# Attention projections 512 columns wide, dealt out behind chosen scores

## The chip, the cores and the metric

The kernel runs on one core of one Trainium2 chip. The metric is the device time of one execution in microseconds (us). Its work is done by TensorE (PE in the profile, with the weight loads shown apart as PEld), VectorE (DVE), ScalarE (ACT), GpSimd (POOL) and SyncE (SP, which here only starts transfers); transfers between memory and the core's on-chip buffer run on 16 DMA engines. Each engine takes its own instructions strictly in the order in which they stand in its program, and waits for the others by semaphores.

## The reference

The program is one inference step of a two-layer streaming trunk over 512 prompt frames and 8 running streams of 16 frames, so 640 rows of width 1024. Layer 0 mixes with a chunked gMLP and a short convolution, layer 1 with a forgetting attention (FoX); each is followed by a SwiGLU feed-forward with a short convolution. The change touches layer 1's attention alone:

```
def _fox_project(x, w_in, b_f, q_norm, k_norm):
    z = x @ w_in
    q, k, v, f = jnp.split(z, [D_C, 2 * D_C, 3 * D_C], axis=-1)
    q = _rmsnorm(q.reshape(b, t, C_HEADS, C_HEAD_DIM), q_norm)
    k = _rmsnorm(k.reshape(b, t, C_HEADS, C_HEAD_DIM), k_norm)
    ...
def _fox_attend(q, k, v, dq, dk, q_pos, k_pos):
    s = einsum('bthd,bshd->bhts', q, k) * (C_HEAD_DIM ** -0.5)
    s = s + swapaxes(dq, 1, 2)[..., :, None] - swapaxes(dk, 1, 2)[..., None, :]
    p = softmax(where(k_pos <= q_pos, s, NEG_INF))
    return einsum('bhts,bshd->bthd', p, v)
```

There are 16 heads of 64. The prompt attends causally to itself in blocks of 128 queries; each stream attends to 256 cached rows and its own 16. The keys and values of the new rows are outputs too, and the attention's output goes through one projection (`w_out_c`) onto the residual stream.

## The kernel before, in words

Activations are kept as 8 chunks of 128 features by 640 rows. For accuracy every large product is taken three times, from a high part (a cast) and a low part (the remainder) of each operand: high by high, low by high, high by low. A weight tile is 128x1024; `weights` loads it on SP's queue, casts it on ACT (L94) and subtracts on DVE (L95). Elsewhere (`weights_added`, `weights_down`) the low part is made as the negated high part on ACT (L103) onto which a DMA from POOL's queue adds the raw weights once more (L104, L122), so that DVE has no part in it.

The attention goes over 4 groups of 4 heads. `project` makes q, k and v of a group, one after the other, each 256 columns wide: 5 blocks of 128 rows times 24 matmuls of 128x256 (L696), so 60 walks and 1440 matmuls in all; ACT evicts each block with the row's norm (L699), and q and k are normed per head (squares on ACT, sums and the products on DVE, the power on POOL, L704 to L710). A weight tile holds the 256 columns for half the features, so a kind has two of them.

Each group has two pairs of heads. `operands` transposes q and k of a pair (L726) and makes for each of its heads four score operands: `qa` and `ka` from ACT (L733, L736), half of `qa` and of `kb` copied to other partitions by DMAs on SP's queue (L734, L737), `qb` and the rest of `ka` from DVE (L735, L738), and the rows of the forget terms by two more DMAs. `stream_operands` does so for the streams (L791 to L798). Then come the steps of the pair in the text's order "b30", "s0", "b31", "o", "b20", "s1", "b21", "b10", "b11", "b00", "b01": b and two digits is `prompt_block` of query block 3 to 0 and head 0 or 1 (score L758 and L759, mask L760, maximum L778, exponential L780, reciprocal L781, scaling L783, transposes L765, copy L768 on DVE for odd blocks or L770 on ACT for even ones, product with v L772), s is a pair of streams, o makes the operands of the second pair. `prompt_end` copies the pair's result out (L750). After the groups stands the output projection, 8 blocks of 128x320 matmuls (`po`, L251).

The text is not the order that runs. A list scheduler sets each engine's static order ahead of time, by the text's position as priority and its own model of when each instruction could start. So matmuls of the next group's projection (for the last group: of the output projection) stand wherever the scheduler saw TensorE free. One construct overrides it: what is written under `tc.issue_after(x)` is held behind instruction x.

Of the kernel before, what the change touches and what calls it, by code (L numbers as in the profile page):

```python
# [53 lines left out]
class Core:  # L54
# [52 lines left out]
    def weights_added(self, src):  # L107
        raw = self.raw()
        self.nc.sync.dma_start(out=raw, in_=src)
        return self.added(self.wp, ("whi", "wlo"), raw, src, 1024, 1024)  # L110
# [453 lines left out]
class Attention:  # L564
# [108 lines left out]
    def project(self, g, h, first, after_q=None):  # L673

        k, nc, io = self.k, self.nc, self.io
        z = []
        for kind in range(3):
            if kind == 1 and after_q is not None:
                after_q()
            us = [k.weights(io["w_c"][g, kind, u]) for u in range(2)]  # L680
            zt = self.zp.tile([P, 5, 256], F32, tag="qk" if kind < 2 else "v", name=k.nm("z"), bufs=3 if kind < 2 else 2)
            z.append(zt)
            bank, out = [], []
            for tb in range(5):
                if tb % 2 == 0:
                    bank.append(self.pj.tile([P, 512], F32, tag="pj", name=k.nm("pj")))
                out.append(bank[tb // 2][:, (tb % 2) * 256:(tb % 2) * 256 + 256])
            walk = [(0, 2), (1, 3), (4,)] if first and kind == 0 else [(tb,) for tb in range(5)]
            for tbs in walk:
                for kc in range(8):  # L690
                    wh, wl = us[kc // 4]
                    hh, hl = h[kc]
                    c = (kc % 4) * 256
                    for tb in tbs:
                        for i, (l, r) in enumerate(((hh, wh), (hl, wh), (hh, wl))):
                            nc.tensor.matmul(out[tb], lhsT=l[:, tb * P:(tb + 1) * P], rhs=r[:, c:c + 256],  # L696
                                             start=kc == 0 and i == 0, stop=kc == 7 and i == 2)
            for tb in range(5):
                nc.scalar.activation(out=zt[:, tb, :], in_=out[tb], func=AF.Copy, scale=self.rt[:, tb:tb + 1])  # L699
            if kind < 2:  # L700
                ss = self.zp.tile([P, 20], F32, tag="ss", name=k.nm("ss"))
                for tb in range(5):
                    sq = self.zp.tile([P, 256], F32, tag="sq", name=k.nm("sq"))
                    nc.scalar.activation(out=sq, in_=zt[:, tb, :], func=AF.Square)  # L704
                    nc.vector.reduce_sum(out=ss[:, tb * 4:tb * 4 + 4], in_=sq.rearrange("p (h d) -> p h d", d=64), axis=AX.X)
                    k.rstd_of(ss[:, tb * 4:tb * 4 + 4], ss[:, tb * 4:tb * 4 + 4], 1.0 / 64)
                zh = zt.rearrange("p t (h d) -> p (t h) d", d=64)
                nc.vector.tensor_tensor(out=zh, in0=zh, in1=ss.unsqueeze(2).broadcast_to([P, 20, 64]), op=ALU.mult)
                if kind == 1:
                    nc.vector.tensor_tensor(out=zh, in0=zh, in1=self.cst[:, O_KN:O_KN + 64].unsqueeze(1).broadcast_to([P, 20, 64]), op=ALU.mult)  # L710
            if kind:
                nc.scalar.dma_start(out=io["o_kv"][kind - 1, :, :, 256 * g:256 * g + 256].rearrange("t p c -> p t c"), in_=zt)
        return z
# [38 lines left out]
    def prompt_block(self, g, pair, hh, i, z):  # L752
# [6 lines left out]
        nc.tensor.matmul(s[:, 0:n], lhsT=qb[0:68, i * P:n], rhs=kb[0:68, 0:n], start=False, stop=True)  # L759
# [26 lines left out]
    def stream_operands(self, g, z):  # L786
# [5 lines left out]
        kt = self.sp.tile([P, 256], F32, tag="kts", name=k.nm("kts"))  # L792
# [21 lines left out]
    def streams_pair(self, g, sp, z, ops):  # L814
# [3 lines left out]
        ck = self.sp.tile([P, 1024], F32, tag="ckv", name=k.nm("ck"), bufs=3)  # L818
        nc.sync.dma_start(out=ck, in_=io["c_k"][g, sp])
        cv = self.sp.tile([P, 1024], F32, tag="ckv", name=k.nm("cv"), bufs=3)  # L820
# [32 lines left out]
        on = self.sp.tile([P, P], F32, tag="on", name=k.nm("on"))  # L853
# [9 lines left out]
def build(ctx, tc, io):  # L863
# [73 lines left out]
    def decay():  # L937
        with ExitStack() as ds:
            k.tp = k.pool(ds, "tmpb", bufs=9)
            at.constants()  # L940
            at.decay(h, ds)
        at.open(es)
    for g in range(4):
        z = at.project(g, h, g == 0, decay if g == 0 else None)
        if g == 3:
            o = [k.split(k.hp, HT_, at.o[c]) for c in range(6)]
        sops = at.stream_operands(g, z)
        at.streams_start(g)
        for pair in range(2):
# [3 lines left out]
            for st in ("b30", "s0", "b31", "o", "b20", "s1", "b21", "b10", "b11", "b00", "b01"):  # L953
# [9 lines left out]
    cut = [6, 6, 6, 6, 6, 4, 4, 4]  # L963
    for ob in (6, 7, 0, 1, 2, 3, 4, 5):
        n = cut[ob]
        w = k.weights(io["w_oc"][ob, :, 0:n * P], n * P)
        ps_ = [at.pj.tile([P, 512], F32, tag="pj", name=k.nm("po")) for _ in range(2)]
# [126 lines left out]
```

## Time and profile before

| | us |
|---|---|
| median of 3 runs (from, to) | 1527.41 (1525.31, 1528.93) |
| the profiled execution | 1525.84 |
| its span, first to last instruction | 1524.0 |
| PE busy | 1471.2 (97%) |
| DVE busy | 1047.9 (69%) |
| ACT busy | 736.9 (48%) |
| POOL busy | 211.1 (14%) |
| mean granted TensorE clock | 0.986 of full speed |

The attention's projections and groups stand between about 670 and 1034 us of the span. Busy time is that in which an engine has an instruction in work; PE's is modelled at its ends, since matmuls are pipelined. A row of the timeline or the chain starts with the time from the span's start and a length in us; behind the names, in brackets, stands the idle time ahead of the instruction and what ended it. Rows of groups have the count (x), the busy time in us and the mean of one in ns.

### The profile page before, as it was taken

The page shows a single profiled execution, that of the slowest core. Times are in us where ns is not written, and L with a number is a line of the kernel's source. Part 1 is how long each engine was busy: PE and PEld are TensorE (multiplying, and loading weights), DVE is VectorE, ACT ScalarE, POOL GpSimd, SP SyncE. Part 2 cuts the span into 40 slices and gives each one's busy share as a digit, 9 for nine tenths or more (in the row PEclk, how much of TensorE's full clock was granted, in tenths as well). Part 3 has the DMA queues.
Part 4 walks back from the last instruction along what each step waited for, and adds up shares of the span by engine and source line. Part 5 has one row for each costly group of instructions (what it writes and reads, how often), then busy time and mean ns, then how long its engine had stood idle before and what let it go on. Part 6 is the DMA issues. An engine that isn't in the chain of part 4 may idle for free.

```text
span 1524.0 us, 26325 instructions
## 1 busy us (share of the span) xinstructions
PE 1471.2 (97%) x10576; PEld 1418.3 (93%) x10576; DVE 1047.9 (69%) x1805; ACT 736.9 (48%) x1326; POOL 211.1 (14%) x235
## 2 busy tenths in 40 slices
PE   8999997899999999999999999999699999999998
PEld 6999997899999999989988888888699999999998
DVE  6555438777877777586666657668777686868764
ACT  5422325555555555445544445435455555545551
POOL 4100121101010101135101111003111010101010
PEclk9999998999999999999999999999899999999999
DMA  7222203444444444453534333432254454545342
GB/s 269 77 76 67 67 29 82 133 112 115 106 117 101 115 108 114 81 171 130 171 111 145 109 110 103 161 105 73 54 144 98 99 127 99 127 98 127 97 103 81
DMA packets 74249, 168.04 MB, mean 110 GB/s; under 512 B 13760, under 2 KB 22896, under 8 KB 74000
## 3 DMA queue, kind: packets, MB, share of 16 engines
q1 hardware_dynamic: 49392, 133.79, 27.9%
q0 software_dynamic: 12032, 25.17, 10.4%
q10 hardware_dynamic: 12704, 7.41, 1.6%
q8 instruction: 83, 1.36, 0.4%
q14 instruction: 38, 0.31, 0.1%
HBM read 150.58 MB, written 11.54 MB: 106 GB/s over the span
## 4 chain that ended last, share of the span: by engine, by line
PE 90%; DVE 3%; issue 2%; DMA 2%; ACT 2%; SPq 0%; POOL 0%; DVEq 0%; POOLq 0%
PE mm L251 37%; PE zx L201 20%; PE pj L696 11%; PE aux L201 8%; PE pv L772 3%; PE po L251 2%; PE pt L765 1%; DVE hl L282 1%; PE mm L389 1%; DVE wlo L95 1%; DMA wlo<-w_up 1%; PE pt L851 1%; PE sc L758 1%; PE sc L759 1%; PE scs L830 1%
## 5 line engine op out<-in xcount | busy, mean ns | idle before, releaser
L135 ACT CAST sh<-raw 128x1024 fp32r<-128x1024 f32 (+2 forms) x152 | 142.4, 943 | 192.3 <-PE zx L201 105.4
L251 PE MATMUL mm<-sh,wlo 128*128 128x320 f32 x872 | 203.5, 310 | 5.9 <-ACT sn L216 3.1
L251 PE MATMUL mm<-sh,whi 128*128 128x320 f32 x872 | 200.9, 310 | 2.7 <-ACT sh L135 1.7
L251 PE MATMUL mm<-sl,whi 128*128 128x320 f32 x872 | 199.1, 309 | 0.6 <-DVE sl L136 0.6
L136 DVE TENSOR_TENSOR sl<-raw,sh 128x1024 fp32r<-128x1024 f32 (+2 forms) x152 | 165.0, 1091 | 45.2 <-ACT sh L135 31.0
L348 DVE SCALAR_TENSOR_TENSOR t<-zp,cst,t 128x656 f32<-128x656 f32 x184 | 163.6, 896 | 29.1 <-ACT t L346 28.5
L201 PE MATMUL zx<-hh,sh 128*128 128x320 f32 x576 | 178.2, 309 | 2.0 <-ACT sh L135 1.3
L201 PE MATMUL zx<-hl,sh 128*128 128x320 f32 x576 | 177.8, 309 | 0.0
L201 PE MATMUL zx<-hh,sl 128*128 128x320 f32 x576 | 177.6, 308 | 0.0
L251 PEld LDWEIGHTS mm<-sh,wlo 128*128 128x128 f32 x872 | 147.5, 189 | 6.4 <-ACT sn L216 3.3
L94 ACT CAST whi<-raw 128x1024 fp32r<-128x1024 f32 (+3 forms) x94 | 80.1, 856 | 149.6 <-PE mm L251 85.8
L251 PEld LDWEIGHTS mm<-sh,whi 128*128 128x128 f32 x872 | 146.3, 188 | 4.6 <-ACT sh L135 2.4
L251 PEld LDWEIGHTS mm<-sl,whi 128*128 128x128 f32 x872 | 146.1, 188 | 1.1 <-DVE sl L136 1.1
L696 PE MATMUL pj<-whi,hl 128*128 128x256 f32 x480 | 137.3, 287 | 3.1 <-DVE hl L282 3.1
L359 DVE TENSOR_TENSOR x<-mm,x 128x640 f32<-128x640 f32 x111 | 91.2, 822 | 69.3 <-PE mm L251 69.0
L696 PE MATMUL pj<-wlo,hh 128*128 128x256 f32 x480 | 137.2, 286 | 0.0
L696 PE MATMUL pj<-whi,hh 128*128 128x256 f32 x480 | 136.7, 287 | 0.0
L251 PE MATMUL mm<-hh,whi 128*128 128x320 f32 x512 | 120.3, 317 | 10.4 <-ACT whi L102 10.4
L251 PE MATMUL mm<-hh,wlo 128*128 128x320 f32 x512 | 118.5, 314 | 10.9 <-DMA wlo<-w_up 10.9
L251 PE MATMUL mm<-hl,whi 128*128 128x320 f32 x512 | 119.4, 315 | 2.0 <-DVE hl L282 2.0
L95 DVE TENSOR_TENSOR wlo<-raw,whi 128x1024 fp32r<-128x1024 f32 (+3 forms) x94 | 101.6, 1084 | 23.5 <-ACT whi L94 23.3
L201 PEld LDWEIGHTS zx<-hh,sh 128*128 128x128 f32 x576 | 108.5, 188 | 2.8 <-ACT sh L135 1.5
(232 smaller groups left out, 3350.5 us busy)
## 6 DMA issues: line engine op xcount, KB each, us to landing
raw<-w_up SPq DMA_DIRECT2D x88, 512.0 KB
raw<-w_dn SPq DMA_DIRECT2D x40, 512.0 KB
wlo<-w_dn POOLq DMA_DIRECT2D x40, 512.0 KB, 5.9
raw<-w_c SPq DMA_DIRECT2D x24, 512.0 KB
raw<-w_ab SPq DMA_DIRECT2D x16, 512.0 KB
ck<-c_k SPq DMA_DIRECT2D x16, 512.0 KB
cv<-c_v SPq DMA_DIRECT2D x16, 512.0 KB
o_kv<-z ACTq DMA_DIRECT2D x8, 640.0 KB
```

Of the source, the lines that this page charges most:

```text
L94: nc.scalar.copy(out=hi[:, c], in_=raw[:, c])
L95: nc.vector.tensor_tensor(out=lo[:, c], in0=raw[:, c], in1=hi[:, c].bitcast(F32), op=ALU.subtract)
L135: nc.scalar.copy(out=hi, in_=src)
L136: nc.vector.tensor_tensor(out=lo, in0=src, in1=hi.bitcast(F32), op=ALU.subtract)
L201: nc.tensor.matmul(out, lhsT=l[:, c], rhs=r, start=start and p == 0 and i == 0, stop=p == 3 and i == 2, skip_group_check=True)
L251: nc.tensor.matmul(outs[h], lhsT=l, rhs=r[:, h * HT:(h + 1) * HT], start=start and k == 0, stop=stop and k == 2)
L282: nc.vector.scalar_tensor_tensor(out=lo, in0=x, scalar=gs, in1=hi.bitcast(F32), op0=ALU.mult, op1=ALU.subtract)
L348: nc.vector.scalar_tensor_tensor(out=cv[:, 0:CW], in0=zp[:, i:i + CW], scalar=w[:, i:i + 1], in1=cv[:, 0:CW], op0=ALU.mult, op1=ALU.add)
L359: self.nc.vector.tensor_tensor(out=x, in0=ps[:, C0:C0 + T], in1=x, op=ALU.add)
L389: nc.tensor.matmul(pvs[tb], lhsT=l[:, tb * P:(tb + 1) * P], rhs=r[:, (kc % 2) * 512:(kc % 2 + 1) * 512], start=kc == 0 and k == 0, stop=kc ...
L696: nc.tensor.matmul(out[tb], lhsT=l[:, tb * P:(tb + 1) * P], rhs=r[:, c:c + 256], start=kc == 0 and i == 0, stop=kc == 7 and i == 2)
L772: nc.tensor.matmul(ov[64 * hh:64 * hh + 64, i * P:n], lhsT=z[2][:, j, (2 * pair + hh) * 64:(2 * pair + hh) * 64 + 64], rhs=u[:, j * P:(j + ...
```

## The change

q and k of a group are projected together, 512 columns wide (`project_qk`), and v of two groups together (`project_v`). A walk is one block of 128 rows by 512 columns: 24 matmuls of 128x512. There are 4 x 5 walks for q and k and 2 x 5 for v, less joined ones in the first group, so 720 matmuls. Each projection has four weight tiles, each with the 512 columns for a quarter of the features; the buffers stay at five for the high and five for the low parts. The first group's q and k and the first v are projected ahead of the loop with `weights`; the other 16 tiles and the 8 of the output projection now come by `weights_added`.

The rest of the projection and the output projection's blocks are no longer left to the scheduler's filling. They are 28 steps in `queue`, and the tables `share` and `after` say behind which scores of which pair the next step's TensorE work is held: two, three or four steps for a pair, never one behind b00 or b01 and none ahead of b30. Eviction and norms are now per walk and 512 wide; a q and k tile is normed in one product of 2560 columns on DVE. Some buffer counts change.

```
-    def weights_added(self, src):
+    def weights_added(self, src, cols=1024):
...
+        return self.added(self.wp, ("whi", "wlo"), raw, src, 1024, cols)
-    def project(self, g, h, first, after_q=None):
...
-                if tb % 2 == 0:
-                    bank.append(self.pj.tile([P, 512], F32, tag="pj", name=k.nm("pj")))
...
-                            nc.tensor.matmul(out[tb], lhsT=l[:, tb * P:(tb + 1) * P], rhs=r[:, c:c + 256],
...
+    def walk(self, us, h, tbs, evict):
+        k, nc = self.k, self.nc
+        out = [self.pj.tile([P, 512], F32, tag="pj", name=k.nm("pj")) for _ in tbs]
+        for kc in range(8):
+            wh, wl = us[kc // 2]
+            hh, hl = h[kc]
+            c = (kc % 2) * 512
+            for tb, o in zip(tbs, out):
+                for i, (l, r) in enumerate(((hh, wh), (hl, wh), (hh, wl))):
+                    nc.tensor.matmul(o, lhsT=l[:, tb * P:(tb + 1) * P], rhs=r[:, c:c + 512],
+                                     start=kc == 0 and i == 0, stop=kc == 7 and i == 2)
+        for tb, o in zip(tbs, out):
+            evict(tb, o)
+
+    def project_qk(self, g, h, pairs=False):
...
+        zt = self.zp.tile([P, 5, 512], F32, tag="qk", name=k.nm("z"), bufs=2)
+        ss = self.zp.tile([P, 40], F32, tag="ss", name=k.nm("ss"))
+
+        def evict(tb, o):
+            nc.scalar.activation(out=zt[:, tb, :], in_=o, func=AF.Copy, scale=self.rt[:, tb:tb + 1])
+            sq = self.zp.tile([P, 512], F32, tag="sq", name=k.nm("sq"), bufs=1)
+            nc.scalar.activation(out=sq, in_=zt[:, tb, :], func=AF.Square)
+            s = ss[:, tb * 8:tb * 8 + 8]
+            nc.vector.reduce_sum(out=s, in_=sq.rearrange("p (h d) -> p h d", d=64), axis=AX.X)
+            k.rstd_of(s, s, 1.0 / 64)
+            if tb < 4:
+                return
+            zh = zt.rearrange("p t (h d) -> p (t h) d", d=64)
+            nc.vector.tensor_tensor(out=zh, in0=zh, in1=ss.unsqueeze(2).broadcast_to([P, 40, 64]), op=ALU.mult)
+            zk = zt[:, :, 256:512].rearrange("p t (h d) -> p t h d", d=64)
+            nc.vector.tensor_tensor(out=zk, in0=zk, in1=self.cst[:, O_KN:O_KN + 64].unsqueeze(1).unsqueeze(1).broadcast_to([P, 5, 4, 64]), op=ALU.mult)
+            nc.scalar.dma_start(out=io["o_kv"][0, :, :, 256 * g:256 * g + 256].rearrange("t p c -> p t c"), in_=zt[:, :, 256:512])
+        us = []
+        def step(tbs):
+            if not us:
+                us.extend((k.weights_added if g else k.weights)(io["w_qk"][g, u]) for u in range(4))
+            self.walk(us, h, tbs, evict)
+        walk = [(0, 1), (2, 3), (4,)] if pairs else [(tb,) for tb in range(5)]
+        return (zt[:, :, 0:256], zt[:, :, 256:512]), [lambda tbs=tbs: step(tbs) for tbs in walk]
+
+    def project_v(self, gg, h):
+
+        k, nc, io = self.k, self.nc, self.io
+        zs = [self.zp.tile([P, 5, 256], F32, tag="v", name=k.nm("z"), bufs=3) for _ in range(2)]
+
+        def evict(tb, o):
+            for i, zt in enumerate(zs):
+                nc.scalar.activation(out=zt[:, tb, :], in_=o[:, 256 * i:256 * i + 256], func=AF.Copy, scale=self.rt[:, tb:tb + 1])
+                if tb == 4:
+                    g = 2 * gg + i
+                    nc.scalar.dma_start(out=io["o_kv"][1, :, :, 256 * g:256 * g + 256].rearrange("t p c -> p t c"), in_=zt)
+        us = []
+        def step(tb):
+            if not us:
+                us.extend((k.weights_added if gg else k.weights)(io["w_vc"][gg, u]) for u in range(4))
+            self.walk(us, h, (tb,), evict)
+        return zs, [lambda tb=tb: step(tb) for tb in range(5)]
+        score = nc.tensor.matmul(s[:, 0:n], lhsT=qb[0:68, i * P:n], rhs=kb[0:68, 0:n], start=False, stop=True)
+        return score
...
+    cut = [6, 6, 6, 6, 6, 4, 4, 4]
+    def out_block(ob):
+        n = cut[ob]
+        w = k.weights_added(io["w_oc"][ob, :, 0:n * P], n * P)
+        ps_ = [at.pj.tile([P, 512], F32, tag="pj", name=k.nm("po")) for _ in range(2)]
+        for kc in range(n):
+            k.mm([p_[:, 0:HT] for p_ in ps_], w, kc, o[kc], kc == 0, kc == n - 1)
+        if ob < 6:
+            nc.sync.dma_start(out=x[ob], in_=io["s_x"][ob])
...
+    qk, steps = at.project_qk(0, h, True)
+    for f in steps:
+        f()
+    decay()
+    v, steps = at.project_v(0, h)
+    for f in steps:
+        f()
+
+    share = {(0, 0): 3, (0, 1): 4, (1, 0): 4, (1, 1): 4, (2, 0): 3, (2, 1): 2, (3, 0): 4, (3, 1): 4}
+    after = {2: ("b30", "b21"), 3: ("b30", "b31", "b21"), 4: ("b30", "b31", "b21", "b11")}
+    qks = {}
+    queue = []
     for g in range(4):
-        z = at.project(g, h, g == 0, decay if g == 0 else None)
-        if g == 3:
+        z = qk + (v[g],)
+        if g == 0:
+            for i in (1, 2):
+                qks[i], steps = at.project_qk(i, h)
+                queue += steps
+            vs, steps = at.project_v(1, h)
+            v += vs
+            queue += steps
+        elif g == 1:
+            qks[3], steps = at.project_qk(3, h)
+            queue += steps
+        elif g == 3:
             o = [k.split(k.hp, HT_, at.o[c]) for c in range(6)]
+            queue += [lambda ob=ob: out_block(ob) for ob in (6, 7, 0, 1, 2, 3, 4, 5)]
         sops = at.stream_operands(g, z)
...
-                    at.prompt_block(g, pair, int(st[2]), int(st[1]), z)
+                    score = at.prompt_block(g, pair, int(st[2]), int(st[1]), z)
+                    if st in after[share[g, pair]]:
+                        with tc.issue_after(score.ins):
+                            queue.pop(0)()
             at.prompt_end(g, pair)
...
-        w = k.weights(io["w_oc"][ob, :, 0:n * P], n * P)
...
+        qk = qks.get(g + 1)
+    assert not queue
```

Left out are the smaller buffer counts (q and k tiles 3 to 2 of double width, v tiles 2 to 3, cached rows `ckv` 3 to 2, `kts` and `on` 2 to 1) and the new packing of the weights ahead of the run. In the changed program's numbering the score's two matmuls are L777 and L778, the operand transposes L745, `qa` L752, `ka` L755, the stream operands L811 and L818, the probabilities' transposes L784, the products with v L791, the projection L683, and the evictions L695 (q, k) and L723 (v).

Three places show how the engines' programs change; rows are "line, operation, output, inputs, shape", and the numbers in the names tell tiles apart.

On TensorE before, from the end of group 0 to the first score of group 1 (`pt_1125` and `pt_1126` take the transposed q and k of the new pair, `pj` is the projection, `sc` the score):

```order
L772 MATMUL pv_1014_7619<-u_1080_7865,z_921_7154 64x128
L726 MATMUL pt_1125_8366<-cst_66,z_1087_7881 128x128
L726 MATMUL pt_1126_8371<-cst_66,z_1103_8049 128x128 x4
L696 MATMUL pj_1287_8948<-whi_1280_8935,hl_815_6447 128x256
...
L696 MATMUL pj_1288_8949<-whi_1280_8935,hl_808_6419 128x256
L758 MATMUL sc_1136_8401<-ka_1128_8377,qa_1127_8376 128x512
```

Between the last operand transpose and the score stand 46 projection matmuls; at the starts of groups 0 and 2 there are 43 and 37, and at that of group 3 output projection in their place.

The same place on TensorE after the change, from the last two scores of group 0 to the first of group 1:

```order
L777 MATMUL sc_1120_8001<-ka_989_7414,qa_988_7413 128x128
L778 MATMUL sc_1120_8001<-kb_991_7416,qb_990_7415 128x128
L875 MATMUL pt_1077_7814<-cst_66,on_1079_7832 128x128
L791 MATMUL pv_1039_7613<-u_1105_7932,z_907_6988 64x128 x2
L791 MATMUL pv_1039_7613<-u_1111_7950,z_907_6988 64x128 x2
L784 MATMUL pt_1118_7996<-cst_66,p_1115_7989 128x128
L784 MATMUL pt_1124_8012<-cst_66,p_1121_8005 128x128
L811 MATMUL pt_1128_8020<-cst_66,z_926_7151 128x128 x4
L791 MATMUL pv_1039_7613<-u_1119_7998,z_907_6988 64x128
L745 MATMUL pt_1130_8037<-cst_66,z_926_7151 128x128 x4
...
L745 MATMUL pt_1131_8042<-cst_66,z_926_7151 128x128 x4
L777 MATMUL sc_1141_8072<-ka_1133_8048,qa_1132_8047 128x512
```

No projection matmul stands in this stretch any more: the score follows the transposes directly, and so it does at the starts of the other three groups. The next step's matmuls (`pj_1147`) come behind the score's second half.

On ACT after the change, from the next-to-last walk of the first v (`pj_924`) to the first pair's `qa` (`whi_955` to `whi_961` belong to the next q and k, `whi_1087` to the ones after it):

```order
L723 ACTIVATE z_908_6989<-pj_924_7095,rt_853_6598 128x256
L102 CAST whi_955_7240<-raw_954_7238 128x1024 [waits DMAHW2_49,PE_49]
L103 ACTIVATE wlo_956_7241<-whi_955_7240 128x1024 [waits DMASW2_49,PE_49,Activation_49]
L102 CAST whi_958_7247<-raw_957_7245 128x1024 [waits PE_49]
L102 CAST whi_961_7254<-raw_960_7252 128x1024 [waits PE_49]
L103 ACTIVATE wlo_959_7248<-whi_958_7247 128x1024 [waits DMASW7_49,Activation_49]
L102 CAST whi_1087_7861<-raw_1086_7859 128x1024 [waits DMAHW5_49,PE_49]
L103 ACTIVATE wlo_962_7255<-whi_961_7254 128x1024 [waits DMASW6_49,Activation_49]
L723 ACTIVATE z_907_6988<-pj_925_7122,rt_853_6598 128x256 [waits PE_49]
L723 ACTIVATE z_908_6989<-pj_925_7122,rt_853_6598 128x256
L752 ACTIVATE qa_936_7184<-pt_934_7174,qn8_6619 64x512 [waits DMAHW0_49,DMAHW7_49,DVE_49,PE_49]
```

Seven casts and negations of weights stand ahead of `qa`; before, `qa` of the first pair stood directly behind the eviction of an earlier walk of v, with no weight cast between. `PE_49` in the brackets is the release of the weight buffer, which the last walk of v still reads.

More of the change, by code (lines that the diff above doesn't have):

```diff
@@ L105, in added @@
         return hi, lo
-    def weights_added(self, src):
-        raw = self.raw()
+    def weights_added(self, src, cols=1024):
+        raw = self.raw()[:, 0:cols]
         self.nc.sync.dma_start(out=raw, in_=src)
-        return self.added(self.wp, ("whi", "wlo"), raw, src, 1024, 1024)
+        return self.added(self.wp, ("whi", "wlo"), raw, src, 1024, cols)
     def weights_down(self, src, n):
```

63 lines of the change are left out of this document (11 added, 52 removed).

## The prediction

> **What bounds the kernel now.** I read the busy times first, then the chain of work that ended last, then busy time by stretches around the attention.
>
> ```profile
> PE 1471.2 (97%) x10576; PEld 1418.3 (93%) x10576; DVE 1047.9 (69%) x1805; ACT 736.9 (48%) x1326; POOL 211.1 (14%) x235
> PE 90%; DVE 3%; issue 2%; DMA 2%; ACT 2%; SPq 0%; POOL 0%; DVEq 0%; POOLq 0%
> ```
>
> TensorE is busy for 97% of the span and makes 90% of the chain. The stretches (columns: from and to, length, then busy time and count on PE, PEld, DVE, ACT and POOL, granted clock, DMA share, GB/s) say where it is not:
>
> ```profile
> 670.00:685.00 15.00, 12.12 (x84) 11.07 (x83) 15.00 (x10) 8.32 (x12) 13.38 (x11) 1.00 0.32 112
> 685.00:978.00 293.00, 290.84 (x2590) 260.54 (x2591) 194.86 (x523) 146.59 (x352) 50.52 (x47) 1.00 0.42 131
> 978.00:1034.00 56.00, 55.42 (x483) 47.24 (x482) 39.13 (x129) 20.91 (x62) 0.17 (x3) 0.98 0.29 93
> ```
>
> The attention's start waits for VectorE (15.00 of 15). From 685 to 1034 us TensorE is idle 2.16 + 0.58 = 2.7 us. So work off TensorE is worth nothing there: whatever ACT or DVE save is not on the chain. The change can win only by cheaper matmuls and the start, and lose by every wait that it opens.
>
> **What it wins.** The chain shows how fast each form goes back to back (start, length, line, count):
>
> ```profile
> 694.52 17.28 PE pj L696 x144
> 712.45 14.39 PE pj L696 x120
> ...
> 31.86 2.72 PE mm L389 x12
> 36.17 2.73 PE mm L389 x12
> ```
>
> The 128x256 form takes 17.28/144 = 0.120 us. A 128x512 form of the same weights by rows exists in layer 0: 2.72/12 = 0.227 us. The projections go from 1440 x 0.120 = 172.8 to 720 x 0.227 = 163.4 us: **-9.4**.
>
> [...]
>
> At the start, the high and low parts of the input come from DVE chunk by chunk:
>
> ```profile
> 677.70 0.38 PE L696 MATMUL pj<-whi,hl 128*128 128x256 f32 x1 [1.15 <-DVE hl L282]
> ...
> 679.80 0.39 PE L696 MATMUL pj<-whi,hl 128*128 128x256 f32 x1 [0.25 <-DVE hl L282]
> ...
> 681.91 0.38 PE L696 MATMUL pj<-whi,hl 128*128 128x256 f32 x1 [0.23 <-DVE hl L282]
> ```
>
> These waits and one behind them are within the 15.00 - 12.12 = 2.9 us idle there. Twice the work per chunk (q and k at once) fills them: **-2.9**; bounds 0 (DVE as late as the work is longer) and -2.9.
>
> At the start of group 3 the filling output projection was itself late:
>
> ```profile
> 970.11 1.49 ACT L798 ACTIVATE qbd<-pt,qn 64x128 f32<-64x128 f32 x4 [1.89 <-DVE kts L793]
> ...
> 971.63 0.59 ACT L750 COPY x<-pv 128x512 f32<-128x512 f32 x1
> ...
> 972.24 0.68 ACT L733 ACTIVATE qa<-pt,qn 64x512 fp32r<-64x512 f32 x1
> ...
> 972.95 0.54 SPq L734 DMA_DIRECT2D qa<-qa  x1
> ...
> 974.07 0.56 PE L251 MATMUL po<-sh,whi 128*128 128x320 f32 x2 [1.24 <-ACT sh L135]
> ...
> 975.34 0.47 PE L758 MATMUL sc<-ka,qa 128*128 128x512 f32 x1 [0.71 <-DVE sl L136]
> ```
>
> That is 1.24 + 0.71 = **-2.0**, since no output projection stands there any more. Together -14.3. Fewer changes between forms may give something that no row isolates; the projection's weight loads lose a little to issue, which bounds it at 3 x 1.8 = 5.4 (one row of three alike):
>
> ```profile
> L696 PEld LDWEIGHTS pj<-wlo,hh 128*128 128x128 f32 x480 | 91.5, 191 | 2.0 <-issue 1.8
> ```
>
> I take 0.
>
> **What it loses at the three changes of group.** Before, 46 projection matmuls (5.5 us) stood between the operand transposes and the first score. After, nothing does, and the last two blocks b00 and b01 of the group have no step behind them either. The 128-wide softmax chain:
>
> ```profile
> L780 ACT ACTIVATION_READ_ACCUMULATOR p<-sc,m 128x1 f32 x64 | 12.7, 198 | 0.0
> L778 DVE TENSOR_REDUCE m<-sc 128x1 f32<-128x128 f32 x16 | 4.5, 287 | 0.2
> L780 ACT ACTIVATE p<-sc,m 128x128 f32<-128x128 f32 x16 | 5.9, 370 | 6.4 <-DVE m L778 5.3 <-PE pt L765 0.9
> L783 DVE TENSOR_SCALAR p<-p,l 128x128 f32<-128x128 f32 x16 | 4.4, 284 | 0.3
> L781 DVE RECIPROCAL l<-l 128x1 f32<-128x1 f32 x80 | 12.1, 157 | 7.7 <-ACT p L780 7.0 <-ACT pp L780 0.2
> ```
>
> With a mask as long as the maximum, 0.29 + 0.29 + 0.37 + 0.20 + 0.16 + 0.28 = 1.6 us, and about 0.4 more for the second head: 2.0 from score to probabilities, which stand ahead of the new transposes on TensorE. Then the rows above: qbd 1.49, the pair's copy 0.59, `qa` 0.68, and 975.34 - 972.95 = 2.4 from the issue of its DMA to the score, 5.2 together. Of 7.2, TensorE's own products and transposes in the stretch (some 20 small ones) cover 1.1 to 1.8. Idle: 5.4 to 6.1, I take **6 each, +18**. Bounds: with qbd and the copy behind `qa`, 2.0 + 0.7 + 2.4 - 1.8 = 3.3 each, 10; with nothing covered and, in group 3, the norm of its q and k not yet done (a product of 2560 columns is two of the row below), 3 x 7.2 + 3.0 = 25.
>
> ```profile
> L708 DVE TENSOR_TENSOR z<-z,ss 128x1280 f32<-128x1280 f32 x8 | 11.9, 1485 | 2.6 <-POOL ss L302 2.6
> ```
>
> **What it loses at the first group.** Seven casts and negations of weights now stand ahead of `qa` on ACT:
>
> ```profile
> L94 ACT CAST whi<-raw 128x1024 fp32r<-128x1024 f32 x60 | 62.5, 1048 | 109.8 <-PE mm L251 67.2 <-issue 27.0 <-DMA raw<-w_ab 6.5
> L699 ACT ACTIVATE z<-pj,rt 128x256 f32<-128x256 f32 x60 | 25.7, 472 | 37.1 <-PE pj L696 32.1 <-DVE ss L301 3.5 <-DMA t<-sel 1.3
> L103 ACT ACTIVATE wlo<-whi 128x1024 fp32r<-128x1024 f32 x8 | 8.4, 1054 | 0.0
> ```
>
> Their buffers come free over the last walk of v (24 x 0.227 = 5.4 us), the fourth at its end. From there: a cast 1.05, a negation 1.05, two evictions 0.94, `qa` 0.68, its DMA 2.4 = 6.1; TensorE has 1.8 of transposes. Idle 4.3, and the score's second half waits for `ka` behind qbd; I take **+5**. Bounds: 3 if the fourth buffer is free earlier, 7.4 if all seven run after the walk and only transposes lie beside them.
>
> **Weights.** Four tiles a projection and five buffers: a new tile can be made only while the old projection's last walk runs. At each of the turnovers inside the queue a tile costs a cast 1.05, a negation 1.05, the POOL issue and the landing:
>
> ```profile
> L122 POOL DMA_DIRECT2D wlo<-w_dn x40 | 48.3, 1208 | 177.4 <-ACT wlo L121 167.5 <-ACT t L495 9.9
> wlo<-w_dn POOLq DMA_DIRECT2D x40, 512.0 KB, 5.9
> wlo<-w_up POOLq DMA_DIRECT2D x8, 512.0 KB, 8.3
> ```
>
> 1.05 + 1.05 + 5.9 = 8.0 us if the landing counts from the issue (9.2 with the issue's 1.2), against the 5.4 us of a walk and the attention's own work until the next step. From qk1 to qk2 about 2.5 late; from qk2 to v1 the last step of the one (behind b11) and the first of the other (behind b30) have a change of group between them. I take **+3**; bounds 0 and 7. Behind a waiting cast on ACT stand exponentials, so a late release delays a softmax too.
>
> [...]
>
> **Uncovered blocks.** Pairs with two or three steps leave b31 or b20, b10, b11 without cover: (0,0), (2,0), (2,1). Two or three chains of the 1.6 to 2.0 us above, partly beside other blocks: **+5**, bounds 0 and 9.
>
> **The clock after waits.**
>
> ```profile
> 970.00:980.00 10.00, 8.05 (x50) 5.51 (x48) 5.88 (x12) 5.59 (x11) 0.00 (x0) 0.83 0.39 109
> 1095.00:1105.00 10.00, 2.02 (x8) 1.62 (x7) 9.52 (x17) 4.37 (x6) 2.93 (x4) 0.50 0.92 207
> ```
>
> Around the group-3 start the clock was granted at 0.83 of full speed for 10 us, a loss of 1.7 us, though TensorE was idle only 2 us there; after a long wait it was 0.50. Four such starts: 4 x 1.7 = **+7**, bounds 0 and 14 (twice as long). [...]
>
> **Sum.** -14.3 + 18 + 5 + 3 + 5 + 7 = +23.7 against the profiled execution's 1525.84 (its span of 1524.0 and 1.8 around it, 1.6 below the median): **1549.5 us**.
>
> **Rivals.** *The waits are hidden and it is faster:* the changes of group cost nothing because the scheduler's transposes and the operands' chain run ahead of b00 and b01, wherever ACT is free: it is 48% busy. Against it: on TensorE the transposes stand behind the last probabilities. It decides once all waits together are under 14.3 us; with the lower bounds, 10 + 3 = 13, less 5.4 for issue, it ends at 1525.84 - 14.3 + 13 - 5.4 = 1519. Chance 0.22. *The same:* lower bounds without the gain from issue, 1524.5; chance 0.06. *Weights late everywhere:* at four turnovers the whole 9.2 us show, +37 instead of +3: 1584. For it: the 8.3 us landing; against: the DMA engines' share is 0.42 in the row of 685 to 978. Chance 0.07. [...] The forecast itself: 0.64.
>
> **The numbers.** The forecast's own range takes lower and upper bounds of half the terms: 1532 to 1570. The range must reach into the faster case: 1518 to 1580. A measurement of this kernel can tell 0.2%, about 3 us, from no change. Faster: 0.22 + 0.01 and a little of the forecast's low side; same 0.07; slower 0.70.
>
> **What would show it.** The new projection's group at 227 ns a matmul in the chain (200 or less: the gain is larger). Idle TensorE of 5 to 6 us ahead of the score at each of three changes of group, released by `qa` or its DMA, and about 5 at the first; under 3 each and the forecast is wrong towards faster. Waits for `wlo` of a few us at the turnovers, 8 or more at each for the slow rival. A granted clock under 0.9 in the 10 us after each start. The forecast fails above all if the stretches without a projection matmul are shorter than the row-by-row chain makes them.

## The result

The changed kernel takes 1588.13 us (1586.04 to 1591.7) against 1527.44 before: a ratio of 1.0401, interval 1.0377 to 1.0425. It is slower, as forecast, but by 61 us and not by 24, outside the range. The profiled execution has a span of 1589.9 against 1524.0.

The busy times and the chain by engine, after:

```profile
PE 1486.7 (94%) x9856; PEld 1391.9 (88%) x9856; DVE 1020.3 (64%) x1737; ACT 752.8 (47%) x1310; POOL 221.4 (14%) x239
PE 78%; DMA 6%; DVE 6%; issue 5%; ACT 3%; POOL 1%; SPq 0%; ACTq 0%; POOLq 0%; DVEq 0%
```

TensorE's share of the chain falls from 90 to 78%. The attention alone, one row for it in each trace (from and to, length, busy time and count on PE, PEld, DVE, ACT, POOL, clock, DMA share, GB/s), first before, then after:

```profile
665.00:1038.00 373.00, 367.00 (x3212) 326.43 (x3212) 254.65 (x669) 180.81 (x433) 66.19 (x64) 1.00 0.40 125
```

```profile
666.00:1102.00 436.00, 380.82 (x2493) 298.53 (x2492) 226.77 (x601) 197.39 (x418) 77.31 (x68) 0.91 0.48 132
```

63 of the 66 us lie here. TensorE has 719 fewer matmuls and yet is busy 14 us longer, because the clock is granted at 0.91; and it is idle 55 us instead of 6. Taken apart from the first projection matmul to the last product with v: idle time, time that TensorE was busy but the clock withheld (the clock records summed over its busy time), and the rest, its work at full clock. The same sums for the experiments stand beside them.

| kernel | ratio to before (interval) | stretch | idle | clock | work |
|---|---|---|---|---|---|
| before | 1 | 372.0 | 6.0 | 1.7 | 364.3 |
| after | 1.0401 (1.0377 to 1.0425) | 434.9 | 55.2 | 24.2 | 355.5 |
| dealt_subtract | 1.0271 (1.0249 to 1.0293) | 412.2 | 38.2 | 18.8 | 355.2 |
| copies_on_act | 1.0434 (1.0408 to 1.0461) | 437.0 | 60.1 | 21.8 | 355.0 |
| operands_before_v | 1.0312 (1.0288 to 1.0337) | 416.1 | 42.3 | 17.9 | 355.9 |
| dealt_start_step | 1.0195 (1.0178 to 1.0212) | 399.1 | 31.5 | 15.9 | 351.7 |
| dummies_at_starts | 1.0383 (1.0361 to 1.0405) | 433.3 | 34.7 | 21.2 | 377.3 |
| dealt_not_held | 1.0112 (1.0092 to 1.0133) | 388.5 | 21.6 | 11.1 | 355.8 |
| wide_filled_added | 1.0116 (1.0100 to 1.0133) | 387.7 | 21.5 | 10.9 | 355.2 |
| wide_filled | 1.0061 (1.0046 to 1.0076) | 384.9 | 19.6 | 10.1 | 355.2 |
| before_added | 1.0066 (1.0050 to 1.0082) | 382.1 | 10.5 | 5.1 | 366.4 |
| wide_qk_v_per_group | 1.0061 (1.0048 to 1.0075) | 380.1 | 15.0 | 6.7 | 358.4 |
| wide_qk_paced | 1.0050 (1.0037 to 1.0064) | 386.5 | 19.3 | 7.2 | 360.0 |
| wide_qk_paced_front | 1.0078 (1.0060 to 1.0096) | 387.8 | 18.2 | 9.3 | 360.3 |
| first_group_narrow | 1.0017 (1.0002 to 1.0032) | 374.8 | 9.9 | 1.7 | 363.1 |
| before_first_wide | 0.9965 (0.9954 to 0.9976) | 371.9 | 8.1 | 1.7 | 362.1 |

After against before: work -8.8, idle +49.2, clock +22.5, together +62.9. What lies ahead of this stretch and behind it does the same work in every version, yet takes from 1147 to 1158 us in these traces; so a difference of a few us in the ratio need not come from the attention. The profiled execution of dealt_subtract was the fastest of its four, 7 us under their median.

The main waits of TensorE in the timeline of after:

```profile
678.50 0.50 PE L683 MATMUL pj<-whi,hl 128*128 128x512 f32 x1 [2.35 <-DVE hl L282]
...
680.61 0.50 PE L683 MATMUL pj<-whi,hl 128*128 128x512 f32 x1 [0.45 <-DVE hl L282]
...
682.71 0.50 PE L683 MATMUL pj<-whi,hl 128*128 128x512 f32 x1 [0.44 <-DVE hl L282]
...
758.37 0.77 PE L777 MATMUL sc<-ka,qa 128*128 128x512 f32 x1 [18.32 <-DMA qa<-qa]
...
822.30 0.50 PE L683 MATMUL pj<-wlo,hh 128*128 128x512 f32 x1 [1.08 <-DMA wlo<-w_qk]
...
837.23 0.50 PE L784 MATMUL pt<-cst,p 128*128 128x128 f32 x2 [1.87 <-DVE p L803]
...
844.45 0.65 PE L777 MATMUL sc<-ka,qa 128*128 128x512 f32 x1 [2.91 <-DVE qb L754]
...
880.47 0.80 PE L683 MATMUL pj<-wlo,hh 128*128 128x512 f32 x1 [3.90 <-DMA wlo<-w_vc]
...
933.59 0.84 PE L784 MATMUL pt<-cst,p 128*128 128x128 f32 x2 [1.90 <-DVE l L801]
...
943.87 0.77 PE L777 MATMUL sc<-ka,qa 128*128 128x512 f32 x1 [5.26 <-DMA qa<-qa]
...
1011.36 0.49 PE L784 MATMUL pt<-cst,p 128*128 128x128 f32 x2 [1.16 <-DVE p L803]
...
1015.78 0.66 PE L811 MATMUL pt<-cst,z 128*128 128x128 f32 x2 [2.83 <-DVE z L704]
...
1022.39 0.80 PE L777 MATMUL sc<-ka,qa 128*128 128x512 f32 x1 [3.02 <-DVE ka L757]
...
1057.57 0.52 PE L784 MATMUL pt<-cst,p 128*128 128x128 f32 x3 [1.63 <-DVE o L879]
```

The three changes of group are the pairs at 837 and 844, 934 and 944, and the three at 1011 to 1022: 4.8, 7.2 and 7.0 us, 19.0 together. The first group's start alone is 18.3, and its releaser is the copy of `qa`. SyncE's queue there with ACT's `qa` among it, and what SyncE's issues waited for (us in total, times, longest):

```profile
740.84 1.35 SPq L109 DMA_DIRECT2D raw<-w_qk  x3
...
742.25 0.67 ACT L752 ACTIVATE qa<-pt,qn 64x512 fp32r<-64x512 f32 x1
...
743.08 0.33 SPq L109 DMA_DIRECT2D raw<-w_vc  x1
743.73 0.55 SPq L753 DMA_DIRECT2D qa<-qa  x1
...
747.66 0.49 SPq L756 DMA_DIRECT2D kb<-ka  x1
```

```profile
SPq L760 <- DMA raw<-w_qk: 3.8, 1, 3.8
SPq L753 <- DMA raw<-w_qk: 3.6, 1, 3.6
SPq L756 <- DMA raw<-w_qk: 2.8, 1, 2.8
```

ACT delivered `qa` at 742.25 + 0.67 = 742.9; its copy was issued at 743.73, and the score began at 758.37, 14.6 us later. Four weight loads had gone out just ahead, four accumulating transfers and two writes of v beside them. The windows of these 20 us, and the transfers from 736 to 760 us by queue (packets, MB, share of the 16 engines' time) and by issue:

```profile
740.00:750.00 10.00, 0.05 (x1) 0.00 (x0) 2.79 (x4) 8.34 (x14) 2.65 (x3) 0.61 1.04 246
750.00:760.00 10.00, 1.63 (x14) 0.88 (x18) 0.00 (x0) 0.00 (x0) 0.00 (x0) 0.50 1.05 330
```

```profile
q0 software_dynamic: 576, 2.10, 47.2%
q1 hardware_dynamic: 1010, 2.60, 30.4%
q10 hardware_dynamic: 1263, 1.27, 15.0%
...
wlo<-w_qk POOLq DMA_DIRECT2D x4, 512.0 KB, 8.6
raw<-w_qk SPq DMA_DIRECT2D x3, 512.0 KB
o_kv<-z ACTq DMA_DIRECT2D x2, 640.0 KB
raw<-w_vc SPq DMA_DIRECT2D x1, 512.0 KB
qa<-qa SPq DMA_DIRECT2D x2, 128.0 KB
```

The DMA engines are full (a share of 1.04 and 1.05 in these windows). The accumulating transfers (q0, POOL's queue) take 47.2% for 2.10 MB. Per byte that is nearly twice what SyncE's queue takes (q1, the loads and the small copies): 30.4% for 2.60 MB.

Where the copy's 14.6 us went can be read from the records of single DMA packets in the trace. Its first packet, of 2,048 bytes on SyncE's queue, starts at 756.55. By then 501 of the 512 packets (4,096 bytes each) of the four weight loads issued ahead of it on that queue have started. So the copy stood behind the loads for 12.8 us, and the loads took that long beside the other transfers.

### The profile page after: what moved, and what is told of

It reads as the page before. It is cut to its first block, busy times and chain, and to the rows that moved or that the text cites. A ratio compares the mean times of both kernels' runs of the same rounds, so it can differ in the third digit from the quotient of the medians.

```text
span 1589.9 us, 24849 instructions
## 1 busy us (share of the span) xinstructions
PE 1486.7 (94%) x9856; PEld 1391.9 (88%) x9856; DVE 1020.3 (64%) x1737; ACT 752.8 (47%) x1310; POOL 221.4 (14%) x239
## 4 chain that ended last, share of the span: by engine, by line
PE 78%; DMA 6%; DVE 6%; issue 5%; ACT 3%; POOL 1%; SPq 0%; ACTq 0%; POOLq 0%; DVEq 0%
PE mm L251 34%; PE zx L201 19%; PE aux L201 8%; PE pj L683 6%; PE po L251 3%; PE pv L791 2%; DMA qa<-qa 1%; DMA raw<-w_up 1%; PE mm L389 1%; DVE hl L282 1%; DVE wlo L95 1%; PE pt L784 1%; DMA wlo<-w_up 1%; DMA wlo<-w_dn 1%; POOL ss L302 1%
## 5 line engine op out<-in xcount | busy, mean ns | idle before, releaser
L94 ACT CAST whi<-raw 128x1024 fp32r<-128x1024 f32 (+2 forms) x70 | 57.5, 824 | 143.1 <-PE mm L251 85.8
L201 PEld LDWEIGHTS zx<-hl,sh 128*128 128x128 f32 x576 | 108.4, 188 | 1.1 <-DVE hl L136 1.1
L201 PEld LDWEIGHTS zx<-hh,sl 128*128 128x128 f32 x576 | 108.3, 188 | 0.0
L219 POOL COPY zp<-si 128x16 f32<-128x16 f32 x72 | 38.1, 530 | 471.2 <-DVE t L348 345.2
L683 PE MATMUL pj<-wlo,hh 128*128 128x512 f32 x240 | 98.1, 409 | 5.0 <-DMA wlo<-w_vc 3.9
```

Source lines behind the costliest of these rows:

```text
L94: nc.scalar.copy(out=hi[:, c], in_=raw[:, c])
L201: nc.tensor.matmul(out, lhsT=l[:, c], rhs=r, start=start and p == 0 and i == 0, stop=p == 3 and i == 2, skip_group_check=True)
L219: nc.gpsimd.tensor_copy(out=str_(z)[:, :, 0:2], in_=st.rearrange("p (s c) -> p s c", c=2))
L683: nc.tensor.matmul(o, lhsT=l[:, tb * P:(tb + 1) * P], rhs=r[:, c:c + 512], start=kc == 0 and i == 0, stop=kc == 7 and i == 2)
```

## The experiments

**1. No accumulating DMAs, the order as changed.**

```
-                us.extend((k.weights_added if g else k.weights)(io["w_qk"][g, u]) for u in range(4))
+                us.extend(k.weights(io["w_qk"][g, u]) for u in range(4))
   (and so for v and the output projection)
```

> The changed kernel with the low parts of all weights by VectorE's subtraction again, no accumulating DMA. Traffic theory (the 18.3 us ahead of the first score are four weight loads and four accumulating DMAs that share the DMA engines with the small copies of qa and ka): half the bytes go, the first wait falls from 18.3 to 8 to 11 us, the waits for wlo at the turnovers shrink, 1568 to 1577 us. Cover theory (what is lost is the filling of TensorE's waits by the scheduler, whatever the transfers do): first wait stays over 14 us, 1583 to 1592.

1569.5 us. The first wait is less than half:

```profile
746.87 0.76 PE L777 MATMUL sc<-ka,qa 128*128 128x512 f32 x1 [8.41 <-DMA qa<-qa]
```

That is what the traffic theory said. Of the 19 us, 10 are this wait. The traffic is not all that differs there: three loads and not four stand ahead of the copy on SyncE's queue, and ACT makes no negations. The copy's first packet starts at 744.66, when 367 of the 384 packets of these three loads have started. And 42 us remain without an accumulating DMA: the order has a cost of its own.

**2. The copies on another queue.** `nc.sync.dma_start` becomes `nc.scalar.dma_start` at L753 and L756.

> The changed kernel with the copies of qa and ka (L753, L756) started from ScalarE's queue instead of SyncE's. If the copies are late because they stand behind the weight loads in SyncE's queue: the first wait falls from 18.3 to 5 to 8 us, 1565 to 1576 us. If the DMA engines are simply full at that time: it stays at 11 to 18 us, 1578 to 1590. ScalarE's own time for 32 issues (about 0.5 us each) may cost a little at each start.

1593.6 us, and the wait is 20.6:

```profile
744.38 8.60 ACTq L753 DMA_DIRECT2D qa<-qa  x1
...
760.50 0.77 PE L777 MATMUL sc<-ka,qa 128*128 128x512 f32 x1 [20.59 <-DMA qa<-qa]
```

So ScalarE's queue is no way round. But the run does not clear the place in a queue of blame. On ScalarE's queue two writes of v stand ahead of the copy, its issue alone takes 8.60 us there (0.55 on SyncE's), and its first packet starts at 758.77, when 1,202 of the 1,280 packets of these writes have started. In all three traces the copy's packets come behind nearly all that was issued before it on its own queue.

**3. The first operands made ahead of the traffic.**

```
     decay()
+    first = at.stream_operands(0, qk), at.streams_start(0), at.operands(0, 0, qk)
     v, steps = at.project_v(0, h)
...
-                pops = [at.operands(g, 0, z), None]
+                pops = [at.operands(g, 0, z) if g else first[2], None]
```

> The changed kernel with the first group's operands (transposes, qa, ka and their copies) made ahead of the first v's walks instead of behind them; transfers and steps as they were. Traffic theory (the first wait of 18.3 us is the small copies beside the weights' turnover): the wait falls under 4 us, the waits of the first turnover for wlo stay or grow a little: 1567 to 1575. If the weights are late in any case (the next step's low parts land as late as 756 us): 1576 to 1588.

1573.9 us, 14 less than after, with every transfer left in. The copy is issued at 738.04, ahead of the four loads (from 743.76) and not behind them. The first wait is 1.3; a wait for weights grows in its place, within what the traffic theory expected:

```profile
740.44 0.47 PE L777 MATMUL sc<-ka,qa 128*128 128x512 f32 x1 [1.30 <-DMA qa<-qa]
...
747.94 0.51 PE L683 MATMUL pj<-wlo,hh 128*128 128x512 f32 x1 [3.80 <-DMA wlo<-w_qk]
```

**4. The hold taken off.**

```
-                        with tc.issue_after(score.ins):
-                            queue.pop(0)()
+                        queue.pop(0)()
```

> The changed kernel without the hold: the 28 steps stand in the text where they did, but the scheduler may place their matmuls anywhere. If the hold is what opens the waits at the starts of groups 1 to 3 (19 us of idle TensorE and most of the 23 us of reduced clock): 1555 to 1570 us. If the waits come from the work placed ahead of the loop and the transfers: 1580 to 1590, as the changed kernel.

1545.4 us, 43 less and better than the theory asked for: idle falls from 55 to 22 us and the withheld clock from 24 to 11. Nothing else changed, so the hold is the largest single part of the loss.

**5. Wide projections filled in, with and without accumulating DMAs.** The queue and its tables are taken out; q and k of a group, and v at every second, are projected at the loop's head as before.

```
     for g in range(4):
+        qk, steps = at.project_qk(g, h, g == 0)
+        for f in steps:
+            f()
+        if g == 0:
+            decay()
+        if g % 2 == 0:
+            (v of groups g and g + 1 by project_v, all steps)
```

> The 512-wide projections alone: q and k of a group and v of two groups in the program's text where before had its projection (the scheduler fills TensorE's waits with them), output projection behind the loop, VectorE's subtraction for all weights. Cover theory: no waits over 2 us at the starts, and the wide form's 9.4 us come through: 1515 to 1520 us. If the wide form itself is the loss (larger steps, one evicted bank of 512, norms of 2560 columns): 1530 or more.

> The wide projections filled in by the scheduler, as in wide_filled (1536 us), with accumulating DMAs for the low parts. If the transfers cost the same with either order: some 19 us more (1569.5 against 1588 in the dealt order), 1555. If filling spreads them, as in the kernel before (10 us): 1544 to 1548.

1536.0 and 1545.2 us. The second is within 0.2 us of dealt_not_held, though its steps stand at other places in the text. The accumulating DMAs cost 9 us with filling and 19 with dealing. In the attention alone, by the stretches in the table, it is 2.8 and 22.7; the rest of the 9 lies outside it. So they cost more where no filling stands before the score that waits for the copy. The first is in the second theory's range, but not for the reason that this theory names: the work is 9 us less, as the cover theory had it. TensorE is idle 20 us where before was 6, for the most part from 915 us on.

**6. The kernel before with accumulating DMAs.** `k.weights` becomes `k.weights_added` for groups 1 to 3 and the output projection.

> The kernel before with the low parts of its weights (all but the first group's, and the output projection's) by accumulating DMAs. Traffic theory: the extra 11 MB are spread by the filling order, so 1526 to 1535 us, and any wait shows at turnovers of weights. Cover theory: 1525 to 1529, no difference.

1536.2 us, 10 more, slightly over the range given. Even among the filling of before, the same wait opens:

```profile
745.99 0.55 PE L758 MATMUL sc<-ka,qa 128*128 128x512 f32 x1 [4.68 <-DMA qa<-qa]
```

**7. A step at each start.** On dealt_subtract, the step behind b30 of each first pair is held behind the operands' last transpose instead (and b30 is taken out of the tables for these pairs).

```
                 pops = [at.operands(g, 0, z), None]
+                with tc.issue_after(at.last.ins):
+                    queue.pop(0)()
```

> The changed order with VectorE's subtraction (dealt_subtract, 1569.5 us), and the step behind b30 of each first pair moved ahead of it, between the operands' transposes and the first score. Cover theory for the starts (waits of 8.4, 2.8, 3.6 and 2.9 us there, and reduced clock behind them): 1550 to 1562. If cover that moves only moves the wait (b31 and s0 then lack it): 1564 to 1573.

1557.0 us, 13 less: cover ahead of the first score is worth more than behind it. Part of the wait does move to the next block, as the second theory had it (1.93 and 2.38 us at a score that is released by an earlier block's exponential, `p L801`):

```profile
751.49 0.47 PE L778 MATMUL sc<-ka,qa 128*128 128x512 f32 x1 [2.51 <-DMA qa<-qa]
...
756.37 0.79 PE L778 MATMUL sc<-ka,qa 128*128 128x512 f32 x1 [1.93 <-ACT p L801]
...
838.84 0.79 PE L778 MATMUL sc<-ka,qa 128*128 128x512 f32 x1 [2.38 <-ACT p L801]
```

**8. Unused matmuls in the waits.**

```
+                with tc.issue_after(at.last.ins):
+                    idle = at.pj.tile([P, 512], F32, tag="pj", name=k.nm("idle"))
+                    for i in range(60 if g == 0 else 12):
+                        nc.tensor.matmul(idle, lhsT=h[0][0][:, 0:P], rhs=h[1][0][:, 0:512], ...)
```

> The changed kernel with matmuls added whose result is not used, between the operands' transposes and the first score: 60 of 128x512 (13.6 us at 0.227) at group 0 and 12 (2.7 us) at groups 1 to 3. Clock theory (TensorE idle at a start brings half clock for the work behind it): 1570 to 1582, faster with more work. If the clock costs nothing of its own: 1588 to 1595.

1585.5 us; its interval overlaps that of after. 96 matmuls (21.8 us of work) went in and idle fell by 20.5: free, but no gain. Behind the changes of group the clock is indeed better. Two of them, in after and then with the added matmuls:

```profile
840.00:850.00 10.00, 7.09 (x33) 4.38 (x33) 4.91 (x11) 4.66 (x11) 0.00 (x0) 0.67 0.43 108
...
1020.00:1030.00 10.00, 7.61 (x40) 6.03 (x41) 4.15 (x12) 3.40 (x9) 0.00 (x0) 0.56 0.47 133
```

```profile
840.00:850.00 10.00, 8.46 (x46) 6.25 (x45) 5.40 (x19) 6.75 (x17) 1.67 (x1) 0.83 0.06 14
...
1020.00:1030.00 10.00, 10.00 (x60) 8.14 (x59) 5.17 (x14) 4.95 (x12) 0.00 (x0) 0.83 0.60 183
```

Around the three changes of group the withheld time falls from 16.2 to 8.9 us. Over the whole attention it falls only from 24.2 to 21.2: it stays at 3.8 at the first start, and elsewhere between 770 and 900 us it grows by 4.4, in part beside waits for weights that are longer now (4.24 in place of the 3.90). So work for nothing buys back 3 us of the clock's loss here, and the time can't be told from that of after.

**9. Why the wide form alone is not faster.** First v by group again (no v of group 1 ahead of the loop), then the filling kept from running ahead:

```
-        if g % 2 == 0:  (v of two groups)
+        v.append(at.project_v(g, h))          # 256 wide
```

> q and k of a group 512 wide, but v of each group by itself as before (256 wide, no v of the next group ahead of the loop), filled in by the scheduler, VectorE's subtraction. Cover theory (wide_filled is slower because v of two groups at once takes 13.6 us of filling work out of the loop and leaves group 2 short): the waits of 918 to 990 us go, gain of q and k alone 480 x (2 x 0.120 - 0.227) = 6 us: 1519 to 1523. If the wide steps themselves cost: 1528 to 1536.

1536.8 us, no different from wide_filled. In the traces its attention is 4.8 us shorter, but the idle time of 918 to 990 us, which was to go, is still 10.5 us (12.7 in wide_filled): the cover theory's cause (v of the next group ahead of the loop) explains little of it. TensorE still runs out of filling in group 2. Counted in the static order between a group's first and last score, at 0.227 and 0.120 us a matmul (0.147 for the output projection), 10.5 us of filling stand there against 35.5 before, since 45.9 had been placed in group 1.

```
+    held = (((-1, 1, "b11"), (0, 0, "b30"), (0, 0, "b31"), (0, 0, "b21"), (0, 1, "b30")), (0, 1, "b31"))
+            with tc.issue_after(score of that block):   (group relative, pair, block, for the five walks and v)
                 f()
```

> As wide_qk_v_per_group, and each walk of the next group's q and k, and its v, may not be placed ahead of a given score of this group, so that the filling can't be used up early (static order: 8.2 to 9.7 us of filling ahead of each group's first score and 30 to 33 us within each group, against 15.7, 3.0, 1.2 and 45.9, 10.5 in wide_qk_v_per_group). If filling used up early is what cost 8 us there: idle TensorE falls from 15 to 5 to 7 us, reduced clock from 7 to 2 us, 1519 to 1524. If the wide steps cost otherwise (weights late at turnovers): 1528 to 1537.

1534.7 us, not the 1519 to 1524 of the theory, and the late weights that its rival names are not there either. The idle time of 918 to 990 us falls from 10.5 to 3.9, and more than that comes back at the first score:

```profile
744.57 0.77 PE L782 MATMUL sc<-ka,qa 128*128 128x512 f32 x1 [9.12 <-DMA qa<-qa]
```

There is no accumulating DMA here. q and k of the first group end together and later, their norm is one product behind both, and the first score comes at 744.6 instead of 732.5. Two runs take this apart, the first with the first group's q, k and v one after the other and 256 wide, the second with that group's joint q and k alone in the kernel before:

> As wide_qk_paced (1534.7 us, first wait 9.1), but the first group's q, k and v one after the other, 256 wide, as before; q and k of groups 1 to 3 512 wide. Front theory (q and k of the first group together end later, so their norm, the decay rows and the first score come some 12 us later than before, and filling or idle time pays for it): the first score back at 732 to 736 us, idle TensorE 6 to 9 us, gain of the wide form 360 x (2 x 0.120 - 0.227) = 4.7 us: 1520 to 1525. If the wide steps cost inside the groups: 1529 to 1536.

> The kernel before with only the first group's q and k projected together, 512 wide; all else as before. Front theory: the first score some 10 us later, filled by work that is missing later or idle: 1530 to 1537. If the front costs nothing: 1524 to 1527.

first_group_narrow takes 1528.0 us, by its ratio 0.02 to 0.32% above before and 3 us over the front theory's range, but idle 9.9 where wide_qk_paced had 19.3, and with the score at 734 us:

```profile
734.28 0.47 PE L820 MATMUL sc<-ka,qa 128*128 128x512 f32 x1 [1.82 <-DMA qa<-qa]
```

before_first_wide takes 1521.8 us, against my theory faster than before, by 0.24 to 0.46%. Its first score is as late as the theory said, but the static order has 15 us of filling ahead of it (5 before) and does not lack that later:

```profile
743.79 0.47 PE L791 MATMUL sc<-ka,qa 128*128 128x512 f32 x1 [0.42 <-DVE ss L301]
```

Its attention takes 371.9 us, before's 372.0. The 5 us of its profiled execution come from the feed-forward part behind it (480 us against 486), where two waits are shorter (7.98 and 3.08 us before, 6.11 and none now); why, no run shows. It is the only version below both kernels, and not by anything seen in the attention.

> As wide_qk_paced (1534.7 us), but two of the next group's walks may be placed ahead of the first group's first score (11 us of filling there instead of 5). Front theory: the wait of 9.1 us at the first score falls to 2 to 4 and the reduced clock behind it goes, idle TensorE 9 to 12 us, 1520 to 1528. If the filling used there is missing later in the first group: waits of the same size inside group 0, 1530 to 1536.

1539.0 us: the first wait is 3.75, but waits of 1.1, 0.9 and 3.1 us open in group 0 and at group 1. Filling used at the front is missing later here.

```profile
741.79 0.76 PE L782 MATMUL sc<-ka,qa 128*128 128x512 f32 x1 [3.75 <-DMA qa<-qa]
...
824.50 0.77 PE L782 MATMUL sc<-ka,qa 128*128 128x512 f32 x1 [3.14 <-DMA qa<-qa]
```

So joint q and k in the first group alone, and in the other three alone (paced there), leave the attention within 3 us of before; both together cost 8 to 16. Each uses some of a margin of filling that before has, which is how I read it; why the scheduler places the wide walks earlier is open.

## Why the prediction was wrong

The side was right and so was the cause, waits that lost their filling; the sum was 39 us short in the attention (+62.9 against +23.7). Two terms make 29 of the 39: the wait at the first group and the clock.

- **The wide form, -9.4:** measured -8.8 of work. Right; a walk of 24 takes 5.5 us in after, 0.230 a matmul, against 0.227 in the prediction's row. The 0.01 that the chance of a faster kernel adds to 0.22 stood for a wide form far under 0.227 us; no run shows one, and the runs showed this in its place:

```profile
782.79 5.51 PE pj L683 x24
```

- **The front, -2.9:** wrong; it brought nothing. TensorE waits for the input's low parts for 2.35 + 0.45 + 0.44 = 3.2 us after, and for 3.1 before (the three rows in the prediction and the one below). Twice the work per chunk did not fill these waits.

```profile
685.21 0.38 PE L696 MATMUL pj<-whi,hl 128*128 128x256 f32 x1 [1.45 <-DVE hl L282]
```

- **The changes of group, +18:** 19.0 measured, near the sum, in part by luck. Each is two waits or more, the first for the last blocks' probabilities. The copy of `qa` that the prediction named ends the wait at one of the three; at the others VectorE's `qb` and `ka` come last. At group 3 the norm of 2560 columns did come too late (2.83, `z L704`), which stood in the bound.
- **The first group, +5:** 18.3. This is the step that failed first. The casts were about as costed: `qa` was done 4.2 us after the last walk (742.9 against 738.7), with 3.7 in the sum. What failed is "its DMA 2.4": that row is from a place where the DMA share was 0.39, and the changed order had put four loads, four accumulating transfers and two writes beside the copy. It took 14.6, of which 12.8 behind the loads on its queue. I had counted these transfers as lateness of weights only, and their share from a 293 us average of 0.42. Runs 1 to 3 bear it out: half the wait goes without the accumulating transfers (and with three loads ahead), none on a queue where other transfers stand ahead, nearly all when the copy goes out before the loads. How the 14.6 divide between the order in the queue and the accumulating transfers beside it, no run separates.
- **Weights, +3:** 1.08 + 3.90 = 5.0, within its bounds. The landings, 5.9 us in the sum, took longer here:

```profile
wlo<-w_qk POOLq DMA_DIRECT2D x12, 512.0 KB, 8.8
wlo<-w_vc POOLq DMA_DIRECT2D x4, 512.0 KB, 8.2
```

- **Uncovered blocks, +5:** about 9.7, what is left of the 55.2 after the waits above. Of these, 3.1 lie in group 3 behind 1045 us (1.63 of it in the row at 1057.57), whose pairs the term didn't count.
- **The clock, +7:** +22.5, three times the term and above its bound. I had priced a loss of 1.7 us behind each of the four starts. It is withheld around all of them (0.67 and 0.56 in the rows of experiment 8): 5.1, 5.8 and 5.3 us around the changes of group and 3.8 behind the first group's long wait. Another 2.5 go by the wait for the weights of v and 1.7 by the one at 1057.57, which the term left out.

Of the rivals, "hidden and faster" is refuted by 55 us of idle TensorE. "Weights late everywhere" came nearest in time (1584) but is not what happened: waits for `wlo` are 5 us, and the traffic hurt the small copies instead. Not foreseen either: the wide form for all of q, k and v does not win even where the scheduler fills (1.0061), so the hold (43 us of the 61) and the accumulating DMAs (9 to 19) sit on a change whose gain of 9 us is already used up by later operands and filling that runs out.

## What to carry to other kernels

Filling work is a stock: count for each stretch how much of it stands ahead of the first instruction that waits for a chain of other engines, and don't hold it behind that instruction. Price a small transfer on a chain by what stands ahead of it on its own queue (12.8 of 14.6 us here) and by the DMA share of the microseconds in which it will run (1.04 and 1.05 here, against 0.39 where the row came from), with every transfer that the new order sets free at the same moment, not by a row from a quiet place. And a cheaper matmul form is only worth its difference if what it makes later, here the norm and the first score, is still covered.

## What was not expected of the hardware

In the window of 736 to 760 us the accumulating DMAs took 47.2/2.10 = 22.5% of the engines' time per MB, SyncE's queue of loads and small copies 30.4/2.60 = 11.7%. Packet by packet it is the same: the median packet of 4,096 bytes took 327 ns in an accumulating transfer and 173 in a load.

With the engines full (1.04 and 1.05 in the windows), a copy of 128 KB took 14.6 us from issue to use on SyncE's queue, and its packets started only when nearly all of those issued before it on that queue had (501 of 512). ScalarE's queue, with two writes ahead, was no shorter a way: 16.1 us from issue to use, of which the issue held the queue for 8.60. And SyncE's later issues waited there 2.8 to 3.8 us each, by the profile's releasers, for weight loads that they don't read.
